# Loading the first network's tokens transposed, and scaling them by a broadcast row on POOL

## The chip, the core and the metric

The kernel runs on one core of a Trainium2 chip. A core has five engines with queues of their own that are worked in order: TensorE (PE in the profile, its weight loads PEld), VectorE (DVE), ScalarE (ACT), GpSimd (POOL) and SyncE (SP, which here only issues transfers). The metric is the device time of one execution in microseconds. The time before is the median of 3 runs.

## What is computed

The reference is two blocks of a network on 256 tokens of width 1024. The change touches only the input of the first feed-forward network of the first block, which runs on the 256 tokens `x` and on 256 context tokens `ctx` (512 in all):

```
def rmsnorm(x, g):
    y = xf * lax.rsqrt(jnp.mean(xf * xf, axis=-1, keepdims=True) + EPS)
    return (y * g.astype(jnp.float32)).astype(x.dtype)
def modulate(x, shift, scale):
    return x * (1.0 + scale) + shift
def swiglu(x, w_in, w_out):
    gate, up = jnp.split(x @ w_in, 2, axis=-1)
    return (jax.nn.silu(gate) * up) @ w_out
def ffn_half(s, shift, scale, gate, g_pre, g_post, w_in, w_out):
    h = swiglu(modulate(rmsnorm(s, g_pre), shift, scale), w_in, w_out)
    return s + 0.5 * gate * rmsnorm(h, g_post)
...
mod_x = jnp.split((jax.nn.silu(c) @ w_ada[l] + b_ada[l])[:, None, :], N_MOD, axis=-1)
mod_c = jnp.split((jax.nn.silu(c_ctx) @ w_ada[l] + b_ada[l])[None, None, :], N_MOD, axis=-1)
xs = ffn_half(xs, mod_x[0], mod_x[1], mod_x[2], g[0], g[1], w_ff_in[l, 0], w_ff_out[l, 0])
cs = ffn_half(cs, mod_c[0], mod_c[1], mod_c[2], g[0], g[1], w_ff_in[l, 0], w_ff_out[l, 0])
```

After it come the mixer of the first block, its second feed-forward network, and the second block with its experts; they take the rest of the time and are left as they are.

## The kernel before

The products need the normed, modulated tokens with the model dimension on the partitions. The stage of the change is `first_ffn` up to the end of its `for f in range(KT + 1)` loop. It works through the model dimension in eight slices f of 128 rows. For each slice:

- SP loads two halves of the modulation weights (`araw`, 512 KB each, `ada_load`, L261), and every second slice two pieces of `w_ff_in` (`raw`, L499), which are split into a high and a low part: `whi` or `wparts` on ScalarE (L139), `wlo` or `wparts` on VectorE (L140).
- TensorE multiplies the modulation weights with SiLU(c) and SiLU(c_ctx) (`ada_rows_of`, L269, eight matmuls, here called the modulation). VectorE copies the result (`arow`, L271), TensorE makes columns of it (`ada_columns`, L279), and VectorE adds the bias (`mods`, L281) and forms the scale (`coef`, L284).
- TensorE turns the slice: a matmul of the tokens with a diagonal matrix that holds 1/rms transposes and scales 128 tokens at once (`turned`, L235, four matmuls for the 512 tokens, into PSUM `aux`).
- ScalarE applies scale and shift to the turned tokens (`nt`, L537, once for x and once for ctx), and the result is split into `hh` (ScalarE, L139) and `hl` (VectorE, L140).
- TensorE adds the slice's share to four accumulators (`first`, in PSUM `mm` and `at`): 12 products of 128x512, three for each of four columns groups (L145 to L147, `mm3`).

Each 1/rms comes from a sum of squares (`xjunk`, by turns on ScalarE and VectorE) and `rstd`; `diagonal` puts it on a diagonal (`diag`, L209). Before all that 18 matmuls on ones (`busy`, L1746) occupy TensorE while the first loads are on their way.

After the loop the same products go on for the rest of the hidden columns (`ffn_hidden`): `act` is SiLU of the gate half on ScalarE (L407), the product with the other half is VectorE's (L409), and the result is split into `hidh` and `hidl`. Its weights come through `weights` (L130, 1 MB `raw` tiles). Beside it runs `ada_late`, which makes the other modulation vectors on VectorE: SiLU rows `scr` on ScalarE (L292), weights `w_adat` (`araw`, L305), multiply-and-sum `ajunk` (L309).

The code is written slice by slice, and a scheduler puts each engine's queue into a fixed order when the program is built, by its own estimate of when each instruction can go. The queue on SP is in order too: a load that waits for its buffer holds up all loads behind it. Pools are reused: the buffers of `ada_late` take the place of tiles of the stage before.

## Time and profile before

| | |
|---|---|
| median of 3 runs | 1851.28 us (1846.19 to 1853.59) |
| the profiled execution | 1846.9 us, of which the span is 1844.8 us |
| TensorE busy | 1718.4 us, 93% of the span |
| VectorE, ScalarE, POOL busy | 1028.9, 735.6 and 19.0 us |
| granted TensorE clock, mean | 0.923 |
| stage of the change | 0 to 58 us |

The page gives one execution: how long each engine is busy, then the span in 40 slices of 46 us, the chain of work that ended last, and groups of instructions with their mean duration. The stage lies in the first two of these 40 slices, so it is read in the timeline and by stretches. Matmuls overlap, so their start times, not their durations, tell how fast they follow each other. A turning of 128 tokens shows as two records.

### The profile page before, as it was taken

What the parts mean: (1) busy time and instruction counts of PE and PEld (TensorE: products, weight loads), DVE (VectorE), ACT (ScalarE), POOL (GpSimd) and SP (SyncE); (2) the same over time, 40 slices, a digit from 0 to 9 for tenths busy, and PEclk for the clock granted to TensorE, in tenths of its full rate; (3) what the DMA queues carried; (4) which work ended last, traced back from release to release, by engine and by line L of the source; (5) the groups of instructions that cost most, each with busy time, mean ns of one, the idle gap of its engine ahead of it and who ended that gap; (6) DMA issues with size and microseconds to landing.
All of it is one profiled execution on the core that took longest, in us unless ns stands there. A gap on an engine that the chain in (4) does not pass through costs nothing.

```text
span 1844.8 us, 32948 instructions
## 1 busy us (share of the span) xinstructions
PE 1718.4 (93%) x13346; PEld 1281.8 (69%) x13347; DVE 1028.9 (56%) x2493; ACT 735.6 (40%) x1583; POOL 19.0 (1%) x37
## 2 busy tenths in 40 slices
PE   8999999999999999999999989999999878787876
PEld 5788787778988889999998888887974222222222
DVE  4888766769977877775657686866740000000001
ACT  4432223647545677475445664556640000000001
POOL 0000000000000000000000000000010000000000
PEclk9999999999999999999999999999998676657677
DMA  8666663324422124556542321111899999999996
GB/s 330 235 216 216 229 238 124 109 92 137 150 96 88 70 92 160 183 187 220 187 161 70 123 98 59 48 48 48 321 357 389 409 409 409 408 409 408 408 408 276
DMA packets 98915, 397.77 MB, mean 216 GB/s; under 512 B 12251, under 2 KB 14924, under 8 KB 85196
## 3 DMA queue, kind: packets, MB, share of 16 engines
q1 hardware_dynamic: 91728, 386.97, 55.6%
q10 hardware_dynamic: 5020, 5.04, 0.9%
q0 software_dynamic: 2016, 3.67, 0.7%
q8 instruction: 105, 1.72, 0.4%
q14 instruction: 46, 0.38, 0.1%
HBM read 394.59 MB, written 1.05 MB: 214 GB/s over the span
## 4 chain that ended last, share of the span: by engine, by line
PE 66%; DMA 23%; DVE 6%; ACT 3%; issue 1%; ACTq 0%; SPq 0%; DVEq 0%
PE mm L145 14%; PE mm L147 13%; PE mm L146 13%; DMA raw<-exp_w_gate 7%; DMA raw<-exp_w_down 7%; DMA raw<-exp_w_up 6%; PE at L145 4%; PE a L1361 4%; PE at L146 4%; PE at L147 4%; DMA araw<-w_adat 2%; PE eps L1642 2%; DVE ajunk L309 1%; DVE wlo L140 1%; PE acc L1686 1%
## 5 line engine op out<-in xcount | busy, mean ns | idle before, releaser
L139 ACT CAST whi<-raw 128x512 fp32r<-128x512 f32 x542 | 309.5, 619 | 256.1 <-PE mm L146 123.8
L140 DVE TENSOR_TENSOR wlo<-raw,whi 128x512 fp32r<-128x512 f32 x542 | 356.3, 685 | 89.8 <-ACT whi L139 85.6
L145 PE MATMUL mm<-hh,whi 128*128 128x256 f32 (+1 forms) x784 | 247.6, 317 | 0.4 <-DVE kl L140 0.4
L147 PE MATMUL mm<-hh,wlo 128*128 128x256 f32 (+1 forms) x784 | 246.8, 317 | 0.5 <-DVE wlo L140 0.2
L146 PE MATMUL mm<-hl,whi 128*128 128x256 f32 (+1 forms) x784 | 246.4, 315 | 0.0
L1642 PE MATMUL eps<-raw,xg 128*32 128x256 f32 x2048 | 183.3, 486 | 32.9 <-DMA raw<-exp_w_gate 20.2
L1649 DVE TENSOR_SCALAR scat<-iota,col 128x256 f32<-128x256 f32 x16 | 6.5, 413 | 278.5 <-PE acc L1686 278.5
L1642 PEld LDWEIGHTS eps<-raw,xg 128*32 128x32 f32 x2048 | 61.6, 130 | 140.4 <-issue 62.1
L145 PEld LDWEIGHTS mm<-hh,whi 128*128 128x128 f32 x784 | 147.7, 189 | 14.2 <-issue 3.2
L146 PEld LDWEIGHTS mm<-hl,whi 128*128 128x128 f32 x784 | 147.6, 188 | 11.0 <-issue 1.2
L147 PEld LDWEIGHTS mm<-hh,wlo 128*128 128x128 f32 x784 | 147.1, 188 | 11.0 <-DVE wlo L140 1.3
L1642 PE MATMUL eps<-raw,ehid 128*32 128x256 f32 x960 | 108.6, 549 | 34.3 <-DMA raw<-exp_w_down 33.8
L1690 ACT COPY ys<-eps 128x256 f32<-128x256 f32 x19 | 7.0, 371 | 304.7 <-PE eps L1642 296.2
L309 DVE SCALAR_TENSOR_TENSOR ajunk<-araw,scr 128x512 bf16<-128x512 f32 x160 | 110.2, 689 | 26.8 <-DMA araw<-w_adat 24.8
L145 PE MATMUL at<-hh,whi 128*128 128x512 f32 (+1 forms) x352 | 119.7, 340 | 0.0
L147 PE MATMUL at<-hh,wlo 128*128 128x512 f32 (+1 forms) x352 | 119.4, 339 | 0.0
L146 PE MATMUL at<-hl,whi 128*128 128x512 f32 (+1 forms) x352 | 119.3, 339 | 0.0
L145 PE MATMUL mm<-whi,hidh 128*128 128x512 f32 x264 | 105.5, 400 | 0.4 <-DVE y L431 0.3
L147 PE MATMUL mm<-whi,hidl 128*128 128x512 f32 x264 | 104.8, 398 | 0.5 <-DVE hidl L140 0.4
L146 PE MATMUL mm<-wlo,hidh 128*128 128x512 f32 x264 | 104.8, 397 | 0.0
L1642 PEld LDWEIGHTS eps<-raw,ehid 128*32 128x32 f32 x960 | 24.2, 129 | 116.0 <-DMA raw<-exp_w_down 97.9
L145 PE MATMUL mm<-h2h,whi 128*128 128x256 f32 x328 | 101.6, 310 | 1.7 <-ACT h2h L988 0.9
(593 smaller groups left out, 3358.5 us busy)
## 6 DMA issues: line engine op xcount, KB each, us to landing
raw<-exp_w_gate SPq DMA_DIRECT2D x128, 512.0 KB, 10.2
raw<-exp_w_up SPq DMA_DIRECT2D x128, 512.0 KB, 10.2
raw<-exp_w_down SPq DMA_DIRECT2D x120, 512.0 KB, 10.2
raw<-w_ff_in SPq DMA_DIRECT2D x42, 1024.0 KB, 4.8
raw<-w_in SPq DMA_DIRECT2D x32, 1024.0 KB, 4.7
araw<-w_adat SPq DMA_DIRECT2D x56, 512.0 KB, 4.5
raw<-w_ff_out SPq DMA_DIRECT2D x20, 1024.0 KB, 4.8
raw<-w_fill SPq DMA_DIRECT2D x22, 512.0 KB, 3.5
```

Source lines behind the costliest of these rows:

```text
L139: self.high = self.nc.scalar.copy(out=hi, in_=src)
L140: self.low = (eng or self.nc.vector).tensor_tensor(out=lo, in0=src, in1=hi.bitcast(F32), op=ALU.subtract)
L145: nc.tensor.matmul(out=ps, lhsT=w[0], rhs=x[0], start=first, stop=False)
L146: nc.tensor.matmul(out=ps, lhsT=w[0], rhs=x[1], start=False, stop=False)
L147: nc.tensor.matmul(out=ps, lhsT=w[1], rhs=x[0], start=False, stop=last)
L309: nc.vector.scalar_tensor_tensor(out=junk, in0=raw[:, s], scalar=1.0, in1=self.scr[v][:, s], op0=ALU.mult, op1=ALU.mult, accum_out=part[:, ...
L1361: self.nc.tensor.matmul(out=ps[r], lhsT=w[r], rhs=x[r], start=start, stop=stop)
L1642: nc.tensor.matmul(out=ps[q], lhsT=x(k), rhs=raw[:, j, :], start=(k == 0), stop=(k == KT - 1))
L1649: nc.vector.tensor_scalar(out=sc, in0=self.iota[:, 0:T], scalar1=col[:, 0, e:e + 1], scalar2=col[:, 1, e:e + 1], op0=ALU.is_equal, op1=ALU ...
L1686: nc.tensor.matmul(out=acc[j][:, tt], lhsT=sc[q, tt * 128:tt * 128 + 128], rhs=ys[q], start=False, stop=False)
L1690: nc.scalar.copy(out=ys, in_=ps)
```

## The change

`layout` adds the tokens transposed in memory (`xct`, eight slices of 128 x 512). A new helper in `first_ffn`, also called `turned`, loads slice f into one of three buffers `xt`. The turning matmuls go. In their place the four diagonals are multiplied by a matrix of ones, once, which gives 1/rms of all 512 tokens as a row on every partition; ScalarE copies it to `rrow`. Each slice of `xt` is multiplied by that row, on VectorE for slice 0 and on POOL for the other seven, and `nt` reads `xt`. The first piece of `w_ff_in` is loaded ahead of the first modulation weights, and `araw` has 8 buffers in place of 10.

```diff
-        raw = [pool.tile([128, 4, 256], F32, name="araw", tag="araw", bufs=10) for _ in range(2)]
+        raw = [pool.tile([128, 4, 256], F32, name="araw", tag="araw", bufs=8) for _ in range(2)]
...
-            raws = [self.ada_load(0, tmp)]
...
+            def turned(f):
+
+                t = tmp.tile([128, 2 * T], F32, name="xt", tag="xt", bufs=3)
+                nc.sync.dma_start(out=t, in_=self.A["xct"][f])
+                return t
+
             weights(0)
-            diag = []
+            raws, xt = [self.ada_load(0, tmp)], [turned(0)]
+
+            ps = self.aux([128, 2 * T])
+            r = tmp.tile([128, 2 * T], F32, name="rrow")
             for i in range(4):
...
-                diag.append(self.diagonal(self.rstd(st), tmp))
+                s = slice(i * 128, i * 128 + 128)
+                nc.tensor.matmul(out=ps[:, s], lhsT=self.ones, rhs=self.diagonal(self.rstd(st), tmp), start=True, stop=True)
+            nc.scalar.copy(out=r, in_=ps)
...
                     if f + 1 < KT:
                         raws.append(self.ada_load(f + 1, tmp))
+                        xt.append(turned(f + 1))
                         if f % 2:
                             weights(f // 2 + 1)
                     row = self.ada_rows_of(raws[f], tmp)
-                    ps = self.aux([128, 2 * T])
-                    self.turned(ps, x, f, diag)
+                    (nc.gpsimd if f else nc.vector).tensor_tensor(out=xt[f], in0=xt[f], in1=r, op=ALU.mult)
...
-                        nc.scalar.activation(out=t, in_=ps[:, cut[i]], func=AF.Identity, scale=a[:, i:i + 1],
+                        nc.scalar.activation(out=t, in_=xt[f][:, cut[i]], func=AF.Identity, scale=a[:, i:i + 1],
...
+    A["xct"] = np.ascontiguousarray(xc.T).reshape(KT, 128, 2 * T)
```

The scheduler makes new orders of the queues in this stage. From the first gemm of `ffn_hidden` on, TensorE's order is the same but for two products; the other places that differ are these.

TensorE's queue between the products of one slice and the next (here the modulation and the turning of slice 5, the first products of slice 4, the columns of slice 5). Before:

```order
L147 MATMUL at<-hh,wlo 128x512
L269 MATMUL at<-araw,sc 32x256 x8
L235 MATMUL aux<-diag,sx 128x128 x2
L235 MATMUL aux<-diag,ctx 128x128 x2
L145 MATMUL mm<-hh,wparts 128x512
L146 MATMUL mm<-hl,wparts 128x512
L147 MATMUL mm<-hh,wparts 128x512
L145 MATMUL mm<-hh,wparts 128x512
L146 MATMUL mm<-hl,wparts 128x512
L147 MATMUL mm<-hh,wparts 128x512
L279 MATMUL mm<-four,arow 128x2 x2
```

and in the changed kernel, around the same modulation:

```order
L147 MATMUL at<-hh,wlo 128x512
L269 MATMUL at<-araw,sc 32x256 x4
L145 MATMUL mm<-hh,wparts 128x512 x2
L146 MATMUL mm<-hl,wparts 128x512
L147 MATMUL mm<-hh,wparts 128x512
L146 MATMUL mm<-hl,wparts 128x512
L269 MATMUL at<-araw,sc 32x256 x4
L147 MATMUL mm<-hh,wparts 128x512
L145 MATMUL at<-hh,whi 128x512
L146 MATMUL at<-hl,whi 128x512
L279 MATMUL mm<-four,arow 128x2 x2
L147 MATMUL at<-hh,wlo 128x512
```

The turning is gone, the second half of the modulation stands behind five products, and the columns (L279) stand behind two of the last six products.

ScalarE's queue at the end of the stage, from the activations `nt` of slice 6 (before) or slice 7 (changed) on. Before:

```order
L537 ACTIVATE nt<-aux,mods,coef_496 128x256 x2
L139 CAST hh<-nt 128x256 x2
L292 ACT_TABLE_LOAD
L292 ACTIVATE scr_578<-scr_578 128x1024
L292 ACTIVATE scr_579<-scr_579 128x1024
L606 DMA w_2305<-fpk 128x272
L537 ACTIVATE nt<-aux,mods,coef_538 128x256 x2
L139 CAST hh<-nt 128x256 x2
L139 CAST whi<-raw 128x512 x3
L407 ACTIVATE act<-mm 128x512 x2
L139 CAST whi<-raw 128x512 x2
```

and in the changed kernel:

```order
L547 ACTIVATE nt<-xt,mods,coef_529 128x256 x2
L139 CAST hh<-nt 128x256 x2
L292 ACT_TABLE_LOAD
L292 ACTIVATE scr_569<-scr_569 128x1024
L407 ACTIVATE act<-mm 128x512
L292 ACTIVATE scr_570<-scr_570 128x1024
L407 ACTIVATE act<-mm 128x512
L139 CAST hidh<-act 128x512
L139 CAST whi<-raw 128x512
L139 CAST hidh<-act 128x512
L139 CAST whi<-raw 128x512 x3
```

The table load and the two SiLU rows moved behind the casts of slice 7, and the weight casts `whi` for the next gemm moved from ahead of `act` to behind the first `hidh`. VectorE's queue follows: its first `wlo` there stands behind `hidl`, `ajunk`, `hidl`, `ajunk`, where three stood ahead of the act product.

SP's queue at the end of the stage. Before:

```order
L499 DMA raw<-w_ff_in 128x512 x2
L261 DMA araw<-w_ada 128x1024 x2
L291 DMA scr_578<-c 128x1024
L291 DMA scr_579<-c_ctx 128x1024
L130 DMA raw<-w_ff_in 128x2048 x2
L305 DMA araw<-w_adat 128x1024 x2
L130 DMA raw<-w_ff_out 128x2048 x2
```

and in the changed kernel:

```order
L505 DMA xt<-xct 128x512
L498 DMA raw<-w_ff_in 128x512 x2
L261 DMA araw<-w_ada 128x1024 x2
L505 DMA xt<-xct 128x512
L291 DMA scr_569<-c 128x1024
L291 DMA scr_570<-c_ctx 128x1024
L130 DMA raw<-w_ff_in 128x2048
L305 DMA araw<-w_adat 128x1024 x2
L130 DMA raw<-w_ff_in 128x2048
L130 DMA raw<-w_ff_out 128x2048
```

Each slice has an `xt` load behind its modulation weights, and one of the two 1 MB weight loads for the next gemm moved behind the `w_adat` loads.

## Rows read from the trace of the kernel before

**Rows 1.** The page's busy times: us, share of the span, instructions of each engine

```profile
PE 1718.4 (93%) x13346; PEld 1281.8 (69%) x13347; DVE 1028.9 (56%) x2493; ACT 735.6 (40%) x1583; POOL 19.0 (1%) x37
```

**Rows 2.** Busy times by stretch: stretch, length, each engine, granted clock, DMA, GB/s

```profile
10.00:18.00 8.00, 5.32 (x46) 3.30 (x46) 4.69 (x16) 4.39 (x11) 0.00 (x0) 1.00 1.02 383
33.00:38.00 5.00, 5.00 (x40) 3.67 (x39) 2.69 (x7) 2.34 (x7) 0.00 (x0) 1.00 1.05 420
```

**Rows 3.** Groups of the first 80 us: the turning (busy us, mean ns)

```profile
L235 PE MATMUL aux<-diag,sx 128*128 128x128 f32 x32 | 5.7, 301 | 3.4 <-DVE diag L209 2.9 <-ACT nt L537 0.5
L235 PE MATMUL aux<-diag,ctx 128*128 128x128 f32 x32 | 5.6, 288 | 0.2 <-DVE diag L209 0.2
```

**Rows 4.** Timeline of slice 4: start us, duration us, engine, line, operation

```profile
37.23 0.48 PE L145 MATMUL at<-hh,whi 128*128 128x512 f32 x1
...
37.93 1.02 ACT L537 ACTIVATE nt<-aux,mods,coef 128x256 f32<-128x256 f32 x2 [2.66 <-DVE coef L284]
...
38.80 1.07 PE L269 MATMUL at<-araw,sc 128*32 128x256 f32 x16
38.84 0.70 ACT L139 CAST hh<-nt 128x256 fp32r<-128x256 f32 x2
...
39.80 0.71 PE L235 MATMUL aux<-diag,sx 128*128 128x128 f32 x4
...
40.71 0.47 PE L145 MATMUL mm<-hh,wparts 128*128 128x512 f32 x1
```

**Rows 5.** Timeline, slices 1 (first row) and 5

```profile
21.78 1.02 ACT L537 ACTIVATE nt<-aux,mods,coef 128x256 f32<-128x256 f32 x2 [3.64 <-DVE coef L284]
...
42.54 0.48 PE L145 MATMUL at<-hh,whi 128*128 128x512 f32 x1
...
45.12 0.41 ACT L139 CAST hh<-nt 128x256 fp32r<-128x256 f32 x1
```

**Rows 6.** Groups of ScalarE: a scaled activation from SBUF (busy us, mean ns)

```profile
L1490 ACT ACTIVATE Ws<-Ws,sms 128x256 f32<-128x256 f32 x16 | 7.9, 497 | 0.0
```

**Rows 7.** Timeline at the stage's end, last row VectorE's

```profile
49.27 1.28 ACT L292 ACT_TABLE_LOAD   x1
...
50.56 2.01 ACT L292 ACTIVATE scr<-scr 128x1024 f32<-128x1024 f32 x2
...
55.38 1.66 ACT L139 CAST whi<-raw 128x512 fp32r<-128x512 f32 x3
...
55.54 0.73 PE L145 MATMUL mm<-hh,wparts 128*128 128x512 f32 x2 [0.72 <-ACT hh L139]
...
58.46 0.40 PE L145 MATMUL mm<-hh,whi 128*128 128x512 f32 x1
...
60.55 0.69 DVE L140 TENSOR_TENSOR hidl<-act,hidh 128x512 fp32r<-128x512 f32 x1
```

**Rows 8.** Timeline of SP's queue

```profile
31.93 12.16 SPq L130 DMA_DIRECT2D raw<-w_ff_in  x2
44.19 1.06 SPq L305 DMA_DIRECT2D araw<-w_adat  x2
```

**Rows 9.** Timeline of POOL's splits and of VectorE beside and after them

```profile
1360.82 5.99 POOL L140 TENSOR_TENSOR hm<-hf,hm 128x256 fp32r<-128x256 f32 x8 [4.33 <-ACT hm L139]
...
1366.41 0.55 DVE L1583 TENSOR_TENSOR sel<-top,slotmask 16x128 f32<-16x128 f32 x1
...
1368.25 0.26 DVE L1583 TENSOR_TENSOR sel<-top,slotmask 16x128 f32<-16x128 f32 x1
```

**Rows 10.** Timeline of TensorE after an idle stretch

```profile
813.02 0.94 PE L235 MATMUL at<-diag,sx 128*128 128x128 f32 x6 [2.77 <-DVE diag L209]
```

**Rows 11.** Busy times by stretch, granted clock third from the right

```profile
815.00:816.00 1.00, 1.00 (x7) 1.00 (x6) 0.83 (x3) 1.00 (x4) 0.00 (x0) 0.50 1.04 438
1012.00:1013.00 1.00, 0.28 (x1) 0.28 (x2) 0.96 (x4) 1.00 (x3) 0.00 (x0) 0.83 0.05 20
1019.00:1020.00 1.00, 1.00 (x9) 1.00 (x9) 0.63 (x2) 0.64 (x2) 0.00 (x0) 0.75 0.95 332
```

## The prediction

> **What bounds the kernel now.** I read the page first: TensorE is busy 93% of the span [rows 1], so a change is worth what it does to TensorE's queue in its own stage. The change sits in the first 58 us, so I read the busy time by stretch next. Until 18 us TensorE waits for data (5.32 us busy out of 8.00), later it is full (5.00 out of 5.00) while VectorE and ScalarE are near half and the DMA engines move 420 GB/s [rows 2]. Then I followed one slice in the timeline. A slice is one 128-row piece f of the model dimension; slice 4 shows the pattern. Its modulation columns end where the next product starts, at 37.23; ScalarE scales the turned tokens at 37.93, the casts hh run from 38.84, VectorE's hl follow, and the products of slice 4 start at 40.71 [rows 4]. From 37.23 to 40.71 TensorE is never idle: six products (1.57 us), the eight modulation matmuls of slice 5 (38.80 to 39.80, 1.00), then the turning of slice 5 (39.80 to 40.71, 0.91). The chain columns, nt, hh ends at 38.84 + 0.70 = 39.54, so it takes 2.31 us and hides under 3.48 us. The turning is both work and cover. The next slice starts 5.31 us later (42.54 less 37.23) [rows 4, 5].
>
> **Part 1: the turning goes.** The 64 records of L235 in the stage [rows 3] are 8 per slice and 0.91 us per slice [rows 4]. Those of slices 0 and 1 lie before 18 us, where TensorE waits anyway; the other six give 6 x 0.91 = 5.5 us of queue time. Four ones-matmuls that make the broadcast row come in, also before 18 us.
>
> **Part 2: the cover goes with it.** The order shows the second half of the modulation matmuls moved behind the first products. The chain stays on ScalarE and VectorE: mods, coef, two nt, two hh. Only nt changes, since it reads SBUF and no longer PSUM. A scaled activation from SBUF takes 0.497 [rows 6] against 0.56 now (1.02 for two that overlap, [rows 4]), so I shorten the chain by 0.12 and add 0.06 for the signal to TensorE: 2.25 us. What TensorE still has in between is, by the new order:
> - slices 1, 2: six products and half a modulation, 1.57 + 0.50 = 2.07; stall 0.18 each, 0.4 in all.
> - slices 3 and 5: the columns stand two products later, 1.60; stall 0.65 each, 1.3.
> - slices 4 and 6: cover 2.07, but a weight cast stands between the two nt on ScalarE. Slice 5 of the kernel before shows that chain: 42.54 to 45.12 + 0.41, 2.99 us [rows 5]; less the same 0.07 it is 2.92; stall 0.85 each, 1.7.
> - slice 7: only four products, 1.0; stall 1.25. There was 0.72 of it already [rows 7], so 0.5 more.
>
> That is 3.9 us. Half modulations between products also cost one more change of kind and back in each slice: twelve products in a row take 58.46 - 55.54 = 2.92 us, 0.24 each [rows 7], six between other kinds 1.57 [rows 4], so 0.13 per pair of changes, 0.8 for six slices. Of 5.5 us saved 4.7 come back, and 0.8 are left. Bounds: 2 us left if the chain is 0.2 us shorter, 1 us lost if it is 0.3 longer.
>
> **Part 3: the start.** The fourth diagonal now stands behind two weight splits of 0.69 each on VectorE (the 128x512 form, [rows 7]), and all of slice 0's modulation stands behind the ones-matmul that needs it. One of these splits stood later in the same chain before, so I take 0.5 us later, between 0 and 1.2. This eats most of what part 2 leaves. The multiplication of slice 0 runs on VectorE while TensorE makes the columns; nothing waits for it.
>
> **Part 4: the end of the stage.** This is the largest term. Before, ScalarE did the table load (1.28) and the two SiLU rows (2.01) at 49.27, in a wait, and three weight casts whi for the next matrix at 55.38, ahead of act; the next gemm started at 58.46 with no gap [rows 7]. In the new order the same work stands behind the last hh, and the first whi stands behind table load, row, act, row, act and hidh. At the spacing of these rows (SiLU rows 1.0 each, casts and act of 128x512 0.52, the last cast to its end 0.62) that is 1.28 + 1.0 + 0.52 + 1.0 + 0.52 + 0.52 + 0.62 = 5.5 us from the last hh to the first whi. TensorE has only the last twelve products there, 2.92: a stall of about 2.5 us. Then it does four matmuls (0.95) and needs the first wlo, which on VectorE stands behind hidl, ajunk, hidl, ajunk. VectorE can start these some 0.45 us before that whi is ready; five at 0.61 (0.69 less their overlap) are 3.05 us, so a further stall of 3.05 - 0.45 - 0.95 = 1.65. Together 4.2 us, and TensorE then has no later gap in which to win it back, for it is full right after. Bounds: 2.5, if VectorE gets there earlier, and 5.5.
>
> **Part 5: transfers.** Eight transposed slices are 2.1 MB more, at 420 GB/s [rows 2] 5 us of transfer. Slice 7's modulation weights are used at 49.4 (two slices after 38.80), and the queue had passed them before its entry at 31.93 [rows 8], over 17 us ahead; 5 us later is still in time. The queue on SP is held by three xt buffers: the load of slice f + 3 waits for nt of slice f, and modulation weights, w_ff_in and the SiLU rows stand behind it, three slices (15 us) before use, so I cost it at nothing; if that cover failed, each slice would wait for a slice's loads, 1.6 MB or 4 us. The second matrix of the next gemm was issued at the end of the 12.16 us entry (31.93), ahead of two w_adat loads at 44.19 [rows 8]; now it stands behind them, and they wait for the buffers of slice 7, near 50. It lands some 7 us after, at 58; TensorE needs it only after the 48 matmuls of the first matrix (48 x 0.24 = 11.5 us after the 58 us mark). Hidden.
>
> **Part 6: POOL.** Seven multiplications of 128x512. Half this size took 5.99/8 = 0.75 us on POOL [rows 9], so 1.5 us each, between 0.75 and 2. They start when xt lands. The tightest is slice 1: about 5.3 MB stand ahead of it in the queue, at 400 GB/s from about 5 us on that is 18 us (an estimate), and nt of slice 1 stood at 21.78 [rows 5], so there are over 3 us. Hidden below some 2.6 us, with 0.5 us left for signals. POOL's library instruction moves to the start too; it has until 18 us there, and where it stood before it fitted in front of a wait of 4.33 us for ScalarE [rows 9].
>
> **Part 7: the clock.** The granted clock fell to half (1.2 GHz) after TensorE had been idle for 2.77 us and busy for 0.94 [rows 10], to 0.50 in the microsecond from 815 and for about 4 us in all. From 1012 to 1019 it stayed down nearly 7 us [rows 11]. In the changed kernel two places look like that: 8 to 14 us (only the ones-matmuls are left there) and the two stalls of part 4. Four microseconds at half clock cost up to 2 us of work. I count one of the two: +2.0. Bounds 0 and 6.7. The Trainium skill (TensorE: Matmul & The Clock Gate, What's actually happening) says the default state is the throttled one and activity releases it; the rows at 815 and 1012 agree. By that rule both places would fall and the term would be +4.
>
> **The sum.** -0.8 (parts 1, 2) + 0.5 (start) + 4.2 (end) + 2.0 (clock) = +5.9 us. On the profiled execution, 1846.9, that is 1852.8. The median of the runs is 1851.28, 4.4 above the profiled one, so I put the forecast at 1857: +0.3%, within the 0.5% (9.3 us) that a measurement of this kernel can just tell from no change.
>
> **Rivals.**
> - *The saved work arrives.* ScalarE and VectorE run ahead of the order's worst case, the end hides as before: -5.5 + 0.5 = -5, 1846. For it: TensorE is the bound [rows 1]. Against: the chain of 2.31 us is in the rows, and queues are worked in order. Faster than 0.5% would need more than the whole turning on the path. Chance 0.10.
> - *Slower: the clock falls at both places and stays down as from 1012 to 1019*, 6.7 us each. That costs 3.3 us twice: -0.3 + 4.2 + 6.7 = +10.6, 1862. It decides once the stretch at half clock is over 5 us at both. For it: the emptier first 14 us. Against: 10 to 18 us kept 1.00 with 5.32 us of work in 8 [rows 2]. Chance 0.17.
> - *POOL and VectorE block each other.* VectorE's two-input op on 16x128 took 0.55 beside POOL's work and 0.26 without it [rows 9]. hl has two inputs in SBUF and stands in the chain; seven multiplications that each hold it up by half of 1.5 us give +5 at most, less the 0.5 us that hl has to spare per slice, about +2: 1859. It decides from a hold of 0.5 us. The Trainium skill (SBUF — State Buffer, SBUF: two separate sides) says that the port pair these two engines share is an exclusive lock for a whole instruction; by that rule each collision costs up to a full multiplication, and it speaks against this change. The 0.55 beside 0.26 agrees with it. Chance 0.13.
> - *The change doesn't do what it says:* xt arrives late, as SP is held, and each slice waits for its transfer. One slice of lag is 4 to 5 us on the path, in place of parts 2 and 7: 1851 + 4 + 4.2 = 1859. Against: part 5's slack. Chance 0.05.
>
> **How the numbers follow.** The forecast has 0.55, the rivals 0.10, 0.17, 0.13 and 0.05. The range reaches from 1849 (parts 2 to 4 at their low bounds and no fall of the clock: -2 + 0 + 2.5 = +0.5, on the middle of 1846.9 and 1851.28) to 1864 (the slow rival and 2 us for a late POOL). Faster by over 0.5%: 0.03, out of the first rival. Slower: 0.18, most of the second rival and the tops of the third and fourth. Same: 0.79.
>
> **What would show it.** In the new profile: 0.2 to 0.9 us of idle TensorE before the first product of each slice, put down to ScalarE's hh (part 2); an idle of over 2 us before mm<-hh,whi put down to whi and one of nearly 2 before wlo (part 4); the granted clock below 1.00 near 14 to 20 or 58 to 64 us (part 7); POOL rows near 1.5 us (part 6). Wrong: no idle at the slices, so that hl and hh come earlier than I add up; no stall at 56 to 61; POOL rows over 2.6 us with nt waiting for POOL; a span 5 us shorter.

## The result: 12.6 us slower, and where 8 to 9 of them lie

The changed kernel takes 1861.87 us (median of 7 runs, 1858.63 to 1865.26), the kernel before 1849.24 on the same chip (7 runs, 1845.93 to 1853.59). The ratio is 1.0066, 95% interval 1.0048 to 1.0084, so 9 to 15.5 us slower. The time lies in the predicted range (1849 to 1864), 5 us above the predicted 1857, and outside the 0.5% that I had called likeliest.

To find the place I follow one row that stands in every kernel: the seventh SiLU `act` of the first network, on ScalarE, behind the whole stage of the change and some 70 us of full TensorE work. I call its start **the mark** (the expectations call the row the first activation of the second hidden pair). ScalarE's timeline of the kernel before, then of the kernel after (start us, duration us, engine, line, operation, idle time before it and who ended it):

```profile
131.49 0.60 ACT L407 ACTIVATE act<-mm 128x512 f32<-128x512 f32 x1 [3.13 <-PE mm L147]
```

```profile
142.11 0.60 ACT L407 ACTIVATE act<-mm 128x512 f32<-128x512 f32 x1 [2.50 <-PE mm L147]
```

In these two executions the mark comes 10.6 us later. TensorE's total went the other way: its busy time fell from 1718.4 [rows 1] to

```profile
PE 1708.2 (92%) x13290; PEld 1270.9 (68%) x13291; DVE 1031.1 (55%) x2494; ACT 736.8 (40%) x1584; POOL 27.9 (2%) x44
```

Ten microseconds less on TensorE, and a later end. The stretches show where (stretch, length, busy time of TensorE, weight loads, VectorE, ScalarE, POOL, granted clock, DMA share, GB/s), against [rows 2]:

```profile
10.00:18.00 8.00, 5.74 (x32) 3.47 (x36) 4.64 (x14) 3.12 (x7) 0.00 (x0) 0.55 1.01 397
18.00:24.00 6.00, 4.77 (x22) 2.27 (x19) 1.50 (x5) 1.69 (x4) 2.54 (x2) 0.50 1.03 401
33.00:38.00 5.00, 4.40 (x32) 2.48 (x30) 1.04 (x4) 1.64 (x5) 1.28 (x1) 1.00 0.86 340
58.00:66.00 8.00, 6.41 (x22) 4.47 (x20) 1.86 (x6) 5.95 (x9) 0.00 (x0) 0.79 0.93 355
66.00:74.00 8.00, 5.33 (x23) 4.03 (x23) 7.88 (x18) 5.30 (x10) 0.00 (x0) 1.00 0.33 113
```

There are three kinds of place: 11 to 24 us at half clock (0.50, the 1.2 GHz level), a loop in which TensorE is busy 4.40 us of 5.00 where it had been full, and the end of the stage, 58 to 74 us, where it was full before.

**The loop.** Slice 4 in the timeline of the kernel after; [rows 4] is the same slice before, where TensorE never waited:

```profile
40.37 0.50 PE L279 MATMUL mm<-four,arow 128*128 128x2 f32 x4
40.44 1.28 POOL L540 TENSOR_TENSOR xt<-xt,rrow 128x512 f32<-128x512 f32 x1 [2.63 <-DMA xt<-xct]
...
40.91 0.16 DVE L281 TENSOR_TENSOR mods<-mm,pv 128x4 f32<-128x4 f32 x1 [1.01 <-PE mm L279]
...
41.11 0.63 DVE L284 TENSOR_SCALAR coef<-mods,pv 128x2 f32<-128x2 f32 x1
...
41.84 0.60 ACT L547 ACTIVATE nt<-xt,mods,coef 128x256 f32<-128x256 f32 x1 [3.27 <-DVE coef L284]
...
42.34 0.60 ACT L139 CAST whi<-raw 128x512 fp32r<-128x512 f32 x1
...
43.16 0.60 ACT L547 ACTIVATE nt<-xt,mods,coef 128x256 f32<-128x256 f32 x1
...
44.24 0.73 PE L145 MATMUL mm<-hh,wparts 128*128 128x512 f32 x2 [1.30 <-ACT hh L139]
```

From the columns (40.37) to the products (44.24) the chain takes 3.87 us; TensorE has six products and half a modulation in it and waits 1.30 us for hh. Three things stretch the chain: the weight cast between the two nt, nt at 0.60 from SBUF, and coef, 0.63 us beside POOL's multiplication where it takes 0.23 without.

**The end of the stage.** ScalarE's timeline and TensorE's, after; [rows 7] is before:

```profile
60.65 0.69 ACT L139 CAST hh<-nt 128x256 fp32r<-128x256 f32 x2
61.36 1.28 ACT L292 ACT_TABLE_LOAD   x1
62.65 1.06 ACT L292 ACTIVATE scr<-scr 128x1024 f32<-128x1024 f32 x1
63.61 0.58 ACT L407 ACTIVATE act<-mm 128x512 f32<-128x512 f32 x1
64.09 1.05 ACT L292 ACTIVATE scr<-scr 128x1024 f32<-128x1024 f32 x1
65.04 0.59 ACT L407 ACTIVATE act<-mm 128x512 f32<-128x512 f32 x1
66.03 0.62 ACT L139 CAST hidh<-act 128x512 fp32r<-128x512 f32 x1 [0.40 <-DVE act L409]
66.55 0.61 ACT L139 CAST whi<-raw 128x512 fp32r<-128x512 f32 x1
```

```profile
61.39 0.78 PE L145 MATMUL mm<-hh,wparts 128*128 128x512 f32 x2 [1.59 <-ACT hh L139]
...
67.22 0.50 PE L145 MATMUL mm<-hh,whi 128*128 128x512 f32 x1 [1.19 <-ACT whi L139]
...
69.90 0.50 PE L147 MATMUL mm<-hh,wlo 128*128 128x512 f32 x1 [1.48 <-DVE wlo L140]
```

The first whi stands behind table, row, act, row, act and hidh. TensorE waits 1.19 and 1.48 us, and the twelve products of slice 7, mostly at half clock, reach their end at about 66.0 where 2.92 us at full clock would have ended at 64.3.

### The profile page after: what moved, and what is told of

Same layout as the page of the kernel before. It is cut to its first block, busy times and chain, and to the rows that moved or that the text cites. A ratio compares the mean times of both kernels' runs of the same rounds, so it can differ in the third digit from the quotient of the medians.

```text
span 1860.0 us, 32861 instructions
## 1 busy us (share of the span) xinstructions
PE 1708.2 (92%) x13290; PEld 1270.9 (68%) x13291; DVE 1031.1 (55%) x2494; ACT 736.8 (40%) x1584; POOL 27.9 (2%) x44
## 4 chain that ended last, share of the span: by engine, by line
PE 67%; DMA 21%; DVE 6%; ACT 4%; issue 1%; ACTq 0%; SPq 0%; DVEq 0%
PE mm L145 13%; PE mm L147 13%; PE mm L146 13%; DMA raw<-exp_w_down 7%; DMA raw<-exp_w_gate 5%; DMA raw<-exp_w_up 4%; PE at L145 4%; PE eps L1652 4%; PE a L1371 4%; PE at L146 4%; PE at L147 4%; DMA araw<-w_adat 2%; PE acc L1696 2%; DVE ajunk L309 1%; DVE wlo L140 1%
## 5 line engine op out<-in xcount | busy, mean ns | idle before, releaser
L1652 PEld LDWEIGHTS eps<-raw,xg 128*32 128x32 f32 x2048 | 56.5, 124 | 151.6 <-DMA raw<-exp_w_up 58.0
L1652 PE MATMUL eps<-raw,ehid 128*32 128x256 f32 x960 | 104.6, 530 | 41.8 <-DMA raw<-exp_w_down 41.6
```

The source lines that it names most:

```text
L1652: nc.tensor.matmul(out=ps[q], lhsT=x(k), rhs=raw[:, j, :], start=(k == 0), stop=(k == KT - 1))
```

## The experiments

Three theories stood against each other. *Order* (mine): what TensorE has between the columns and the next products no longer hides the chain, and at the end the SiLU rows stand ahead of the first whi. *Clock*: the emptied start lets the clock fall, and that is what costs. *POOL*: its multiplication holds up VectorE. All times below are read from each kernel's timeline: the start of the first product of slice 1 (P1), from there to slice 7's (P7), and from P7 to the mark. Where a kernel was profiled twice, both executions stand; the others are one execution each. Between the two of the kernel after the loop differs by 0.24 us and the time behind P7 by 1.4, so differences of that size between the others say little by themselves.

| kernel | P1 | P1 to P7 | P7 to mark | ratio to before (95%) |
|---|---|---|---|---|
| before, two executions | 24.44; 29.25 | 31.10; 31.10 | 75.95; 75.97 | 1 |
| after, two executions | 27.09; 28.85 | 34.30; 34.06 | 80.72; 82.12 | 1.0066 (1.0048 to 1.0084) |
| e1 after, turning kept | 28.66 | 34.37 | 80.79 | 1.0052 (1.0032 to 1.0072) |
| e2 after, start kept busy | 24.41 | 35.05 | 82.41 | 1.0042 (1.0028 to 1.0056) |
| e3 after, SiLUs ahead of nt(7) | 27.45 | 35.05 | 76.08 | 1.0024 (1.0008 to 1.0039) |
| e4 after, multiplication on VectorE | 27.48 | 32.71 | 83.00 | 1.0055 (1.0038 to 1.0072) |
| e5 = e2 and e3 | 26.34 | 34.44 | 76.23 | 1.0010 (1.0000 to 1.0019) |
| e6 = e5, rows(f) whole and first | 27.20 | 28.63 | 76.17 | 0.9994 (0.9982 to 1.0005) |
| e9 = e6, casts behind hh | 26.79 | 26.38 | 76.18 | 0.9967 (0.9955 to 0.9979) |
| b1 before, turning of 2 to 7 left out | 28.37 | 27.29 | 77.46 | not comparable |
| b2 before, loads alone added | 25.92 | 34.04 | 82.80 | 1.0042 (1.0027 to 1.0058) |
| b4 before, orders of e9 | 25.53 | 30.48 | 75.85 | 0.9991 (0.9979 to 1.0004) |

### The end of the stage: e3

In the last pass of the loop:

```
+                    if f == KT - 1:
+                        self.ada_rows(pf)
...
+                    with self.tc.issue_after(self.silu.ins) if f == KT - 1 else ExitStack():
...
```

`ada_rows` makes the two SiLU rows and no longer stands in `ada_late`; the nt and splits of the last slice are issued behind the second of them.

> The changed kernel, with one edit: the load of the SiLU table and the two SiLUs of the scr rows stand ahead of nt of the last slice on ScalarE, as in the kernel before, and not behind hh of that slice; four casts of whi then stand ahead of the two activations act. Theory of the queue (mine): the two stalls of TensorE at the end of the stage, 1.19 us before the first whi and 1.48 us before the first wlo, go; ScalarE is idle for 4.18 us before nt(7), so the SiLUs (1.28 + 2 x 1.05) cost nothing there. 2.7 us gained: 8 us behind the kernel before at 140 us, ratio 1.005. Theory of the clock: what the end of the stage costs is the fall to 0.50 from 62 to 65 us, which comes from the idle 2 x 1.6 us at 60 us and stays: the twelve products still take 4.5 us for 2.9, and the gain is 1 us or less if the stalls had lain under it. Rival: the raw weights land too late for the casts, nothing gained.

ScalarE's timeline of this kernel, and the first matmul on the new weights on TensorE:

```profile
56.90 1.28 ACT L292 ACT_TABLE_LOAD   x1
58.20 2.01 ACT L292 ACTIVATE scr<-scr 128x1024 f32<-128x1024 f32 x2
60.76 1.09 ACT L549 ACTIVATE nt<-xt,mods,coef 128x256 f32<-128x256 f32 x2 [0.55 <-DVE coef L284]
61.75 0.69 ACT L139 CAST hh<-nt 128x256 fp32r<-128x256 f32 x2
62.35 1.66 ACT L139 CAST whi<-raw 128x512 fp32r<-128x512 f32 x3
```

```profile
65.64 0.39 PE L145 MATMUL mm<-hh,whi 128*128 128x512 f32 x1
```

No idle before 65.64, none behind it, and the granted clock stays at 1.00 there, with 1.27 us of idle still before P7. P7 to mark is 76.08, 0.13 from the kernel before. One place in one queue costs 4.6 to 6 us: more than the two stalls, because the half clock goes with them. (The four whi casts ahead of act moved with the SiLUs; the run does not part the two.) The loop of this run is 0.75 us longer than in the first execution of the kernel after; the section on POOL comes back to that. The clock theory's expectation for this run, 1 us or less, fails; that the SiLUs cost nothing ahead of nt(7) is right (ScalarE still waits 0.55 for coef).

### The start and the clock: e2, e5, and both kernels once more

```
-START = 18
+START = 23
...
+                self.busy(3)
```

The three stand behind each of the four matmuls with ones.

> The changed kernel, with five more of the empty matmuls at the program's start (23 for 18) and three behind each of the four matmuls with ones, so that TensorE has work from 1.3 to 14 us. Theory of the clock: the granted clock stays at 1.00 from 8 to 24 us, and what ran at 0.50 there comes back: rows(0) 1.94 us for 1.28, columns 1.01 for 0.61, rows(1) and rows(2) 1.08 for 0.64 each, the six products at 20.13 to 24.16 about 1.1 us. About 2.5 us earlier at products(1) (24.5 for 27.1), and the same at 140 us: 8 us behind the kernel before for 10.6; ratio 1.005. Rival, the start is bound by the chain rstd, diag, ones, copy, multiplication and not by TensorE: products(0) at 20.1 as now, under 1 us gained. Against both: an empty matmul that stands in the way of a matmul with ones costs up to 1 us.

In this execution the clock stays at 1.00 over the start and P1 comes at 24.41, 2.7 us earlier than in the kernel after, as expected. But the mark comes at 141.87: the loop is 0.75 us longer, and the clock falls at the end from 65.4 to 72.2 us instead of 61.9 to 65.4. So I put both edits together:

> The two edits of the runs before on one kernel: empty matmuls over the start, and the SiLUs of the scr rows ahead of nt of the last slice. Alone, the first brought products(1) from 27.09 to 24.41 us, as early as in the kernel before, and lost it again at the end of the stage, where the granted clock fell to 0.50 from 65.4 to 72.2 us (10.4 us behind at 140 us); the second brought the mark to 7.1 us behind. Theory that the two are separate costs, one of the clock and one of the queue: products(7) at 59.5, the first gemm 3 us behind it without a stall, no fall of the clock there, 4.5 us behind the kernel before at 140 us, ratio 1.0015. Rival, the fall at the end comes from the idle time of the loop (1.6 us before products(7)) and not from the two stalls behind it: the clock falls again, 3 to 4 us more, 8 us behind, ratio 1.004.

P7 to mark 76.23, no fall at the end: the first theory, and not the rival. The mark is 5.5 us behind before, for 4.5. The odd thing is the start: the same code as in e2, and the clock is at 0.50 from 11.3 to 14.7 and from 21.5 to 24.9 us, P1 at 26.34. Three kernels, two of them (e5 and e6) with the same edits to the start, had now fallen at 17.5 (b2), 18.6 (e6) and 21.5 us (e5). That asks for the control that I had not thought of before: the same kernels once more.

> The kernel before, unchanged, once more with a profile: how far the marks of one execution can be trusted. If the fall of the granted clock at the start belongs to the changed code, products(0) stand at 18.2 us, products(1) at 24.4, the first activation of the second hidden pair at 131.5, and the clock is 1.00 up to 140 us, as in the first profile. If the clock falls now and then whatever the code, as the falls from 17.5, 18.6 and 21.5 us in three kernels with three different starts let one think, this execution may show one too: products(1) 1.5 to 4 us later, and the mark 1 to 4 us later.

> The changed kernel, unchanged, once more with a profile. If its start fixes the clock: 0.50 from about 11 to 24 us again, products(1) at 27.1, 10.6 us behind the first profile of the kernel before at the mark (142.1). If the clock is a matter of the execution: another length of the fall or none, the mark at 139.5 to 142.5. Under either, the two stalls at the end of the stage (about 1.2 and 1.5 us, before the first whi and the first wlo) and the 0.2 to 1.6 us before each slice's products stand as they were.

Busy time by stretch and TensorE's timeline of the kernel before, second execution; in the first the clock was 1.00 from 10 to 18 us [rows 2] and in this stretch:

```profile
18.00:24.00 6.00, 5.60 (x21) 3.57 (x21) 1.18 (x3) 0.95 (x3) 0.00 (x0) 0.50 1.04 410
```

```profile
10.20 1.40 PE L235 MATMUL aux<-diag,sx 128*128 128x128 f32 x8 [3.44 <-DVE diag L209]
...
19.00 1.22 PE L145 MATMUL mm<-hh,wparts 128*128 128x512 f32 x2
...
29.25 0.47 PE L145 MATMUL mm<-hh,wparts 128*128 128x512 f32 x1
```

The unchanged kernel before falls to 0.50 from 11.0 to 14.4 and from 17.8 to 28.0 us, and its P1 comes at 29.25, 4.8 us later than in the profile on which I predicted, and later than either P1 of the kernel after. So the clock falls at the start without the change as well, and the first profile of before was a lucky one: of the fourteen executions read here only that one and e2 have no fall in the first 30 us. Whether the change lengthens it stays open. The five executions with the start of the kernel before (b1, b2 and b4 among them) have 0 to 13.6 us at 0.50 there, the four with the changed start and no matmuls added to it (both of the kernel after, e3, e4) 13.6 to 17.0. Behind P1 the two executions agree to 0.02 us, so P1 to mark is what can be compared: 107.05 and 107.07 before, 115.02 and 116.18 after. **The change costs 8.0 to 9.1 us there**: 3.0 to 3.2 in the loop, 4.8 to 6.2 at the end.

### POOL beside VectorE: e4

```
-                    (nc.gpsimd if f else nc.vector).tensor_tensor(out=xt[f], in0=xt[f], in1=r, op=ALU.mult)
+                    nc.vector.tensor_tensor(out=xt[f], in0=xt[f], in1=r, op=ALU.mult)
```

> The changed kernel, with all eight multiplications on VectorE and none on POOL; a 128x512 fp32 operation with two operands from SBUF takes VectorE 0.69 us where POOL took 1.26 to 1.28. Theory of contention: coef took 0.54 and 0.63 us beside POOL's multiplication for 0.23 without, and two hl 1.31 for 0.76; without POOL these go, three slices gain 0.3 to 0.55 us each: 1.2 us in all, ratio 1.006. Theory of the queue on VectorE: a multiplication ahead of coef or arow holds these up by 0.69 us in some slices, loss of up to 2 us. Mine: the multiplication is done a slice ahead, and either place is hidden but for these: between -1.5 and +0.7 us.

The loop gains 1.35 to 1.6 us (32.71 for 34.06 and 34.30), and coef takes 0.22 to 0.23 us in all eight slices. That has the size of the contention theory, but it does not test it: the scheduler made other orders of all three queues in the loop. On ScalarE the weight cast no longer stands between the two nt of slices 4 and 6. On VectorE a weight split now stands between mods and coef in slices 2, 4 and 6, so that in slice 2 coef ends 0.91 us after the start of mods, where beside POOL it was 0.74 (29.95 to 30.69). VectorE, this kernel:

```profile
30.53 0.16 DVE L281 TENSOR_TENSOR mods<-mm,pv 128x4 f32<-128x4 f32 x1 [1.49 <-PE mm L279]
30.61 0.69 DVE L140 TENSOR_TENSOR wparts<-raw,wparts 128x512 fp32r<-128x512 f32 x1
31.22 0.22 DVE L284 TENSOR_SCALAR coef<-mods,pv 128x2 f32<-128x2 f32 x1
```

The end loses 1 to 2 us more (a stall of 2.2 and one of 2.1, half clock from 66.7 to 73.6), so the whole time can't tell it from the kernel after.

What POOL costs can be read where the orders are the same. From P1 to P7 the two executions of the kernel after, e2 and e3 have one and the same order on TensorE and on VectorE. Beside slice 5 of the kernel after, a multiplication on POOL (48.22) starts behind the end of coef (47.72 + 0.23); in e3 the same one starts 0.01 us behind coef's start:

```profile
48.04 1.32 DVE L284 TENSOR_SCALAR coef<-mods,pv 128x2 f32<-128x2 f32 x1
48.05 1.29 POOL L541 TENSOR_TENSOR xt<-xt,rrow 128x512 f32<-128x512 f32 x1 [5.99 <-DMA xt<-xct]
...
51.20 0.50 PE L145 MATMUL mm<-hh,wparts 128*128 128x512 f32 x1 [1.80 <-ACT hh L139]
```

TensorE's wait there is 1.80 us for 0.70. In slices 2 to 7 coef is held beyond its 0.23 by 1.9 us in all in e3, by 0.7 and 0.6 in the two executions of the kernel after, and the loops take 35.05, 34.30 and 34.06. In e2 (35.05) coef is held by 0.5, and TensorE waits 0.45 and 0.24 us for hl as well. No run takes the multiplications off POOL and keeps the orders, so this price is read from rows and not tested.

### Lost cover, or the order in which it stands: e1, b1, e6, e9

The turning put back, unread:

```
                     row = self.ada_rows_of(raws[f], tmp)
+                    self.turned(self.aux([128, 2 * T]), x, f, diag)
```

> The changed kernel, with the eight slices of turning matmuls put back on TensorE at their old place; nobody reads what they give, so the chain from the transposed load stands as it is. Measured at 140 us, where the first activation of the second hidden pair stands in all kernels, the changed kernel is 10.6 us behind the kernel before. Theory of the cover (mine): the turning only filled time in which TensorE waits for h(f), 0.23 to 1.6 us a slice now, so 8 x 0.91 us of it come back at no cost or 2 us at most in the loop. Theory of the clock: with those matmuls in 8 to 14 us the granted clock stays at 1.00 over the start, and 2 to 3 us come back as well. Together: 7.5 to 10.6 us behind at 140 us, ratio to the kernel before 1.004 to 1.0065. Rival, TensorE's work is what counts in the loop: 7.3 us more, 18 us behind, ratio 1.0105.

The mark is 12.3 us behind before: 1.7 more than the kernel after for 7.3 us of work, outside the range of my theory and far from the rival's 18. The loop reads 34.37 as against 34.30, but 42 of the 64 records of the turning ran ahead of the first product, where TensorE waits, so this says less about the loop than I meant it to. The clock fell at the start in spite of the added work.

The turning left out of the kernel before:

```
+                    if f < 2:
+                        turns.append(self.aux([128, 2 * T]))
+                        self.turned(turns[f], x, f, diag)
+                    ps = turns[f % 2]
```

> The kernel before, with the turning of slices 2 to 7 left out (slices 2 to 7 use what was turned of slices 0 and 1, so the first network computes with other input): 6 x 0.91 us less on TensorE, no transposed load, no multiplication, the ten buffers and the load order as before. Theory of the cover (mine): the work taken away had covered the chain from columns to hh, so the loop gains 1 to 2.5 us of the 5.5, in stalls of 0.3 to 0.9 us before products(2) to products(7). The scheduler puts the second SiLU of the scr rows behind hh of the last slice here too, so that the end of the stage takes back 1 to 2 us. At 140 us between 2 us ahead and 1 us behind the kernel before, ratio 0.999 to 1.0005. Rival, the loads and POOL are what costs, and the loss of cover nothing: 5 us ahead, ratio 0.997.

The loop takes 27.29 us, 3.8 less than before, with idle time of 0.58 before slice 2, 0.69 before slice 7 and none between: a slice takes 4.41 to 4.46 us from slice 3 to 6. That is nearer to the rival's 5 us than to my 1 to 2.5: without the turning the chain still hides, in this order, in which from slice 3 on the modulation mostly stands whole ahead of the products and six of them follow the columns. The end takes back 1.5 us, as I had expected; the mark is 1.6 us behind, outside my range of 2 ahead to 1 behind, for P1 came at 28.37, after 13.6 us of half clock at the start. (The first network has other input here, and so have all later stages; only the times up to the mark are compared.) So the order itself is the thing to change:

```
-                    products(f - 1, (0, 1))
+                    with self.tc.issue_after(self.last.ins) if 1 < f < KT else ExitStack():
+                        products(f - 1, (0,))
...
-                    products(f - 1, (2, 3))
+                    with self.tc.issue_after(self.last.ins) if 1 < f < KT else ExitStack():
+                        products(f - 1, (1, 2, 3))
```

`self.last` is the last matmul of rows(f).

> The kernel with both edits, and a third: on TensorE the eight matmuls rows(f) stand whole ahead of the twelve products of f-1 (slices 2 to 7), where now the second half of them stands among the products, and columns(f) stand behind three of the products instead of six to nine. Theory of the cover (mine): the stall before products(f), 0.7 to 1.7 us a slice, is the chain columns, mods, coef, nt, hh (2.5 to 2.9 us) less what stands behind columns on TensorE; with nine products (2.1 us) and the next rows (0.64 us) behind them the stall is 0.2 us or none, and a slice takes 12 x 0.2325 + 0.64 + 0.5 + 0.3 = 4.2 to 4.6 us for 5.3 of the kernel before: products(7) at 51 to 54 us, 2 to 4 us ahead of the kernel before at 140 us, ratio 0.998. Rival, transfers: 14 MB have to land up to rows(7), at 410 GB/s by 39 us at the earliest, and three buffers of xt and eight of araw hold the queue; if a slice can't go under 5.3 us for that, products(7) at 56 us, 1 us behind, ratio 1.0005. Rival, POOL: a slice of 4.3 us leaves the multiplications (1.28 us) beside mods, coef and hl more often, 0.3 us each.

One slice of e5 on TensorE (the modulation in halves, columns ahead of four products), then one of e9, which has this order too, on TensorE and ScalarE:

```profile
45.09 0.64 PE L269 MATMUL at<-araw,sc 128*32 128x256 f32 x8
...
46.47 0.50 PE L279 MATMUL mm<-four,arow 128*128 128x2 f32 x4
...
47.93 0.64 PE L269 MATMUL at<-araw,sc 128*32 128x256 f32 x8
49.27 0.73 PE L145 MATMUL mm<-hh,wparts 128*128 128x512 f32 x2 [0.70 <-ACT hh L139]
```

```profile
34.68 1.07 PE L269 MATMUL at<-araw,sc 128*32 128x256 f32 x16
...
35.68 0.50 PE L145 MATMUL mm<-hh,wparts 128*128 128x512 f32 x1
...
36.47 0.50 PE L279 MATMUL mm<-four,arow 128*128 128x2 f32 x4
...
37.53 1.09 ACT L556 ACTIVATE nt<-xt,mods,coef 128x256 f32<-128x256 f32 x2 [1.70 <-DVE coef L284]
...
38.53 0.70 ACT L139 CAST hh<-nt 128x256 fp32r<-128x256 f32 x2
...
40.12 0.50 PE L145 MATMUL mm<-hh,wparts 128*128 128x512 f32 x1
```

The same work: in e5 hh ends the idle time before 49.27, in e9 hh is done at 39.23 and TensorE comes to the product at 40.12 without a pause. In e6 the loop falls from 34.44 to 28.63 us with this one edit, by 5.8. Idle time is 3.35 of that (2.33 us for 5.68). The other 2.5 are busy time: half a modulation, some 0.5 us, now stands ahead of P1, and from P1 to P7 there are 22 changes between products and other matmuls in place of 34. Slices alternate between 4.43 and 5.28 us. In slices 2 and 4 TensorE waits for the hl of the second nt, which stands behind a weight cast on ScalarE:

```profile
42.43 0.50 PE L146 MATMUL mm<-hl,wparts 128*128 128x512 f32 x1 [0.58 <-DVE hl L140]
```

Neither transfers nor POOL set a floor at 5.3 us. P7 came later than I expected (55.83 for 51 to 54); the clock was at 0.50 from 18.6 to 25.4 us. The last edit puts those casts behind both hh:

```
+                    if f % 2 and f + 1 < KT:
+                        with self.tc.issue_after(self.high.ins):
+                            casts(f // 2 + 1)
```

> The kernel with rows first, and one more edit: the casts of the next first-layer weights stand behind both hh of an odd slice on ScalarE and ahead of the nt of the even one, where now one of them stands between the two nt of slices 2, 4 and 6 and holds up the second hl by 0.58 us (slices of 5.28 us beside those of 4.43). Theory (mine): slices 2, 4 and 6 go from 5.28 to 4.45 us, 1.7 to 2.5 us in all; 130 us at the mark, 1.5 to 2 us ahead of the kernel before, ratio 0.9985; less the fall of the clock at the start (18.6 to 25.4 us in the run before), if this execution is without it: 128 us and 0.9975. Rival, the loads: a slice of 4.45 us is too fast for araw and xt, rows(f) wait for them and nothing is gained, ratio 0.9994 as now.

All slices at 4.44 to 4.54 us up to slice 6, the loop 26.38, and the mark 2.1 us ahead of the first execution of before and 7.0 ahead of the second; ratio 0.9967. This kernel is faster than the kernel before and than the kernel after.

### The transfers alone, and the orders alone: b2, b4

Eight loads into tiles that nobody reads, and eight buffers for ten, in the kernel before:

```
-bufs=10) for _ in range(2)]
+bufs=8) for _ in range(2)]
...
                         raws.append(self.ada_load(f + 1, tmp))
+                        turned(f + 1)
```

`turned` issues the load of xt as in the change.

> The kernel before, with its turning, and with the eight transposed loads beside it (2.1 MB into three buffers that nobody reads, araw in eight buffers for ten): the transfers and the queue orders of the change alone. On ScalarE the table and the SiLUs of the scr rows stand behind hh of the last slice, with one of them between the two activations act, as in the changed kernel. Theory of the queue (mine): the loop runs as before (0 to 1 us more, products(7) at 55.5 to 56.5), and the end of the stage has two stalls of 1.2 to 1.5 us before the first whi and the first wlo: 2.7 to 4 us behind at 140 us, ratio 1.002. Theory of the clock: a fall as at 62 to 65 us of the changed kernel comes only behind a loop with idle time; here TensorE is full up to the end, so no fall and no more than that. Rival, the bytes cost: rows(f) wait for araw, 1 us a slice in slices 2 to 5, 5 us behind before products(7).

This is the run that I had most wrong. With all its turning in place, the kernel is 11.3 us behind at the mark: the loop 2.9 us longer, the end 6.85. No slice waits for araw, so the bytes are not it; the queues are. In the loop the second half of the modulation stands among the products here as well, and TensorE waits 0.59 us before slice 2 and 1.19 before slice 7; together 1.1 us more than the one wait of the kernel before. The other 1.8 of the 2.9 are no waits: between P1 and P7 TensorE's time without idle is 32.20 us for 30.37, with 34 changes between products and other matmuls for 22. At the end, ScalarE's queue has the SiLUs behind the last hh, and a transfer that it issues (habs) behind those, and TensorE waits for that:

```profile
66.69 1.08 PE L623 MATMUL aux<-habs,w 33*64 33x256 f32 x2 [3.65 <-DMA habs<-zT]
```

The clock falls there from 65.3 to 72.1 us, behind a loop that was nearly full: my condition for the fall was wrong too. A scheduler that plans by its own estimate of when data arrive had put the same work elsewhere because eight loads were added and two buffers taken away (the run does not part the two).

And the orders of e9 with the turning, in the kernel before:

> The kernel before, with the same two orders (rows(f) ahead of the products of f-1, columns behind three of them; casts of the weights behind hh) and with its turning: what these orders are worth without the change. TensorE had no idle time in slices 0 to 6 of the kernel before, so theory (mine): nothing to gain but one stall of 0.73 us before products(7); the mark at 130.5 to 132 us, ratio 0.9993 to 1.0005. Rival, fewer switches between fp32 and fp32r matmuls (each costs 0.1 us of pitch on the rows): 2 us ahead, ratio 0.999.

30.48 us in the loop for 31.10, no stall before P7, ratio 0.9991: nothing that can be measured. The loop's order on TensorE is that of e9 but for the turning; e9 also has the empty matmuls of e2 at its start. With these equal orders the change leaves 0.24% (0.9967 to 0.9991; the intervals meet at 0.9979), some 4 us of the 5.5 that it takes from TensorE.

## Why the prediction was half right

- **What bounds, and part 1: right.** TensorE's queue is the limit. With equal orders the turning is worth 4.1 us in the loop (e9 26.38, b4 30.48).
- **Part 2, the stalls: right in place and cause, too small in sum.** Forecast before slices 1 to 7: 0.18, 0.18, 0.65, 0.85, 0.65, 0.85, 1.25. Measured: 0.23, 0.55, 0.70, 1.30, 0.70, 0.89, 1.59, in all 5.96 us for 4.61. The two that are 0.4 off, slices 2 and 4, are those in which POOL held coef (0.54 and 0.63 for 0.23). In slice 7, 0.34 off, nt starts 0.43 us behind the end of coef (59.22 to 59.65), in slice 5 only 0.10; the trace does not show why. That nt gets shorter from SBUF was wrong: 1.09 us for two, where PSUM gave 1.02. The row that I took (0.497, [rows 6]) is another activation, without a bias.
- **Part 2, the changes of kind: mis-sized by 1.4 us.** From the first product to P7 TensorE's time without idle is 33.62 us in e2 (40.29 less 6.67) and 36.61 before (37.34 less 0.73), both at full clock. That is 3.0 us less, though 5.2 of turning went: 2.2 came back. I had counted 0.8 for halves of the modulation between products; the changes between products and other matmuls are 40 for 28. The loop gave +3.0 to +3.2 us and not -0.8: 1.3 of the difference are the stalls, 1.4 this term, and the rest is turning and half a modulation that stand on the other side of P1.
- **Part 2's meaning: incomplete.** I wrote that the turning is work and cover. b1, e6 and e9 show that the cover is needed only in the order that the scheduler had chosen; with the modulation whole and first, a slice takes 4.4 us without it.
- **Part 3, the start: can't be told.** The first product comes at 20.13 and 20.95 us after, 18.20 and 19.00 before, so about 1.9 later and not 0.5; at P1 the spread of the clock (24.4 to 29.3 before) has covered it. In the second execution 0.95 us of it is POOL, which held coef of slice 0 (1.18 for 0.23). The one pair without a fall, e2 and the first execution of before, has the first product 1.0 us later and P1 at the same time (24.41 and 24.44); e2 has the empty matmuls besides.
- **Part 4, the end: right in its cause; the stalls smaller, and half clock in their place.** Forecast stalls 2.5 and 1.65; measured 1.19 and 1.48 in one execution, 2.23 and 0.70 in the other, each the less, the more of the products ahead of it ran at half clock. With the clock the end cost 4.8 to 6.2 us, for 4.2 here and 2.0 in part 7. e3 shows that all of it, clock included, hangs on that one order.
- **Part 5, transfers hidden: right for the bytes, wrong for the change.** No product waits for xt or araw. But b2 shows that the loads, with two buffers less, bring about orders like those of parts 2 and 4 even without the change.
- **Part 6, POOL hidden: wrong.** In the loop of the kernel after POOL held coef by 0.7 and 0.6 us, in e3 by 1.9, in the same order. It was among the rivals with 2 us, at a chance of 0.13; the rival spoke of hl, and what was held in the chain was mostly coef. e4 has other orders and can't tell the price.
- **Part 7, the clock: half right.** At the end the fall came in each of the six executions that have the SiLUs behind the last hh and the two stalls or the wait for habs, and in none of the four with the SiLUs moved; it cost 2.1 us in the first (4.77 less 1.19 and 1.48). At the start it is there without the change as well, and whether the change lengthens it is not shown. (The fall at 815 us from which I took about 4 us lasted 3.4, from 814.7 to 818.1.)

The sum of +5.9 against 8.0 to 9.1 us from P1 to the mark misses by the loop. That the time still lies in the range is in part luck: its upper end, 1864, was built from a clock that falls at both places and a late POOL, and not from this. The rest of the 12.6 us, some 4, stays open: the start and the 1700 us behind the mark, which take 1711 to 1720 us in these executions with no order among the kernels (1713 and 1720 in the two of the kernel before).

## What to carry to other kernels

Before you take work off a full queue, build the changed program and read where everything else went: here eight loads more and two buffers less moved two SiLU rows behind a chain, and that alone cost more than the saved matmuls were worth; an order that is forced at two or three places turned the same change from a loss into a gain. Keep the work that a chain waits for whole and ahead of the work that is to hide it. And profile the kernel before twice: a stretch in which the granted clock differs between two executions of the same code must not stand in a sum. Last, an edit that lets the scheduler make other orders (e4 here) measures those orders too: compare the orders first.

## What I had not expected of the hardware

**A small VectorE operation waits for the end of POOL's, to a few hundredths of a microsecond.** The kernel after, second execution, POOL and VectorE in one timeline:

```profile
17.79 0.16 DVE L281 TENSOR_TENSOR mods<-mm,pv 128x4 f32<-128x4 f32 x1 [0.51 <-PE mm L279]
17.88 1.26 POOL L540 TENSOR_TENSOR xt<-xt,rrow 128x512 f32<-128x512 f32 x1 [16.37 <-DMA xt<-xct]
17.98 1.18 DVE L284 TENSOR_SCALAR coef<-mods,pv 128x2 f32<-128x2 f32 x1
...
19.20 1.09 ACT L547 ACTIVATE nt<-xt,mods,coef 128x256 f32<-128x256 f32 x2 [4.26 <-DVE coef L284]
```

coef has two elements a partition, starts 0.10 us behind the multiplication and ends at 19.16, 0.02 behind it. In the first execution 30.15 + 0.54 stands against 29.38 + 1.28, and 41.11 + 0.63 against 40.44 + 1.28: 0.03 and 0.02 again. mods, which reads PSUM, takes 0.16 beside POOL as without it. It goes the other way too: POOL took 1.46 us (21.05) where an hl had started first. The Trainium skill (SBUF — State Buffer, SBUF: two separate sides) calls the port pair that the two engines share an exclusive lock for a whole instruction, for VectorE operations with two SBUF inputs or in a two-port mode; the traces agree.

**The same start at two clocks.** The kernel before ran its first 30 us at 1.00 in one execution and 13.6 us of them at 0.50 in another, with the same instructions; TensorE's idle time before its first turning was 2.91 us in the first and 3.44 in the second. With it P1 came 4.8 us later, which is more than most edits here are worth.
